# Two transformer blocks on one core: sums formed with the last products, an input split by halves, loads moved up, work taken off GpSimd

## The chip, the cores and the metric

The kernel runs on one core of a Trainium2 chip. The metric is the device time of one execution in microseconds, lower is better. TensorE (PE) multiplies matrices into PSUM; VectorE (DVE), ScalarE (ACT) and GpSimd (POOL) work element by element; SyncE (SP) issues the DMA transfers. Each engine works through its own list of instructions in order and waits for others by semaphores.

## The reference, cut to what matters

Two blocks follow each other on one sequence of 1024 positions with 1024 features, all in float32.

```python
def first_block(x, ...):                 # one layer
    z = h @ w_in[i]                      # u_pool | q | k | v
    y_pool = pool_mixer(u_pool, w_pool[i], pool_scale[i])   # per group of 128 columns: mean over
                                         # the last 2, 4, 8, 16 positions minus u, then a matmul
    y_attn = sliding_window_attention(q, k, v, attn_sinks[i])
    h = layer_norm(ALPHA * h + concat([y_pool, y_attn]) @ w_out[i])
    h = layer_norm(ALPHA * h + square(relu(h @ w_ff1[i])) @ w_ff2[i])
    return h + sigmoid(h @ w_ple_gate[i] + b) * (p[i] @ w_ple[i])

def hybrid_layer(x, ...):                # one layer, then rms_norm(x) * final_g
    h = modulate(rms_norm(x), shift_mix, scale_mix)
    qa, ka, va, qb, kb, vb = split(h @ w_in)
    oa = chunked_rel_attention(qa, ka, va, rel_bias)
    ob = stick_breaking_attention(qb, kb, vb)
    x = x + gate_mix * (concat([rms_norm(oa) * g_a, rms_norm(ob) * g_b]) @ w_out)
    gate, val = split(causal_depthwise_conv(modulate(rms_norm(x), ...) @ w_up))
    return x + gate_ffn * ((silu(gate) * val) @ w_down)
```

## The kernel before, in words

**Numbers in two parts.** Every float32 operand of a large matmul is kept as a high part (the value rounded to the format fp32r, which TensorE multiplies fast) and a low part (the value minus its high part). A product takes three matmuls: high by high, high by low, low by high. So each operand needs a split: one copy for the high part and one subtraction for the low part. For weights `prep` (line 519) loads a raw tile by SP, lets GpSimd make the high part (`split_h`, line 511) and VectorE, or the engine given as `low`, the low part. `Stream` (line 536) keeps a ring of weight slots full; its `done` frees a slot and calls for the next weight.

**Order of the work.** The kernel doesn't issue its instructions as they stand. [...] Whenever an engine is free it takes among the instructions that are ready the one that stands first in the program. The order so found is issued; waits are then set by what reads and writes what. All instructions therefore carry one line of the profile, L393, and groups are told apart by the names of their tiles. `follows` and `link` (line 250) tell the planner that a new tile lies in the memory of an old one and must come after it.

**Block 1, first part.** x comes transposed in two halves of columns. Four pooling groups follow (`pool_group`, line 748): a unit of the projection (`unit_T`), whose PSUM results ScalarE copies into `u`, then one to four sums of `u` with itself shifted by 1, 2, 4, 8 columns on VectorE, each with a short copy of the first columns (1, 2, 4, 8 of them) on GpSimd, then d = mean - u, its split (high part on GpSimd), and a small matmul (`pool_matmul`). The buffers `sc` for u, the sums and d are a ring of three. Then k, v, and four pairs of heads of attention (`attn1`, line 886), in which GpSimd normalizes the probabilities. From the third weight on all low parts of the weight stream were made by GpSimd (`ws.low = POOL`, line 724).

**v of block 2.** `wino_N` (line 1080) multiplies 1024 by 1024 matrices by Strassen's scheme in Winograd's form: seven products of half matrices. With `parts` = 1 it is used for v of both attentions. Its sequence is j = 1, 2, 5, 7, 6, 4, 3, each in two halves of the inner dimension (x = 0, 1), 14 elements in all; an element needs two operands (`prep_el`), prepared three ahead. After x = 1 four PSUM banks are copied by ScalarE to the tiles `xs(j, tp)`, tp = 0 to 3. When all are there, `gather` (line 1378) forms the results: x6 += x1, x7 += x6, x3 += x6, x3 += x5, x5 += x7, x4 += x7, x7 = x2 + x1, for each tp three sums on GpSimd and four on VectorE. Eight stores to `d_v` follow.

**q and k of block 2.** Their input h3 (eight tiles of 128 by 1024) is split tile by tile (`split_h3`, line 1465): k = 0 to 3 into the tiles `ga` from a hook that runs two elements before the end of v's products, k = 4 to 7 into slots 0 to 3 after them. `start_T` (line 971) computes the first q and k unit, first for columns 0 to 511 of both, then for 512 to 1023, calls for the next two weights, and the stage is flushed. The next stage (`p7`) loads the relative bias, evacuates these units (`q_evac`, `k_evac2`), and runs eight pairs of heads, each with its q and k unit.

**Down projection.** `wino_N` with two parts covers inner tiles 0 to 15 of 22. The last six are plain products in two sets: four tiles (`sets[0]`), then tiles 20 and 21 (`sets[1]`). In the first set, for each of eight row tiles in the order 0, 4, 1, 5, 2, 6, 3, 7, there is a product, `gather` for rows 0 to 3, a load of the residual `d_x` into a raw tile, and res = (res + product) * gate + residual. The tiles 20 and 21 are loaded by `load_k`: the activation `d_r` (split by ScalarE and VectorE) and the weight (multiplied by the gate and split by GpSimd, low part by VectorE). They were called at rows 1 and 3, that is at the third and the seventh of the eight steps, from a ring of two raw tiles which the residuals use as well.

Of the kernel before, what the change touches and what calls it, by code (L numbers as in the profile page):

```python
# [9 lines left out]
F32 = mybir.dt.float32  # L10
F32R = mybir.dt.float32r
AF = mybir.ActivationFunctionType
ALU = mybir.AluOpType
# [6 lines left out]
NT = S // P  # L20
# [14 lines left out]
def f32(ap):  # L35
    return ap.bitcast(F32)
# [51 lines left out]
class Recorder:  # L88
# [161 lines left out]
    def link(self, idx):  # L250

        op = self.ops[idx]
        if op["eng"] == "SYNC":
            op["deps"], op["cost"] = set(self.watch.get(op["watch"], ())), 0.0
            return
        eng, name, args, kw = op["eng"], op["name"], op["args"], op["kw"]
        aps = [(None, x) for x in args if isinstance(x, bass.AP)] + [(k, x) for k, x in kw.items() if isinstance(x, bass.AP)]
        outs, ins = [], []
        for i, (k, x) in enumerate(aps):
            (outs if (k in ("out", "accum_out") or (k is None and i == 0)) else ins).append(x)  # L260
        if not outs:
            raise ValueError(name)
        deps = set()
        for x in ins:
            key, cells = self.region(x)
            tab = self.cells.setdefault(key, {})
            for c in cells:
                w, r = tab.setdefault(c, [None, []])
                if w is not None:
                    deps.add(w)  # L270
                r.append(idx)
        for x in outs:
            key, cells = self.region(x)
            tab = self.cells.setdefault(key, {})
            for c in cells:
                w, r = tab.setdefault(c, [None, []])
                if w is not None:
                    deps.add(w)
                deps.update(r)
                tab[c] = [idx, []]  # L280
        for x in ins + outs:
            key = x.tensor.name
            self.watch.setdefault(key, []).append(idx)
            if key in self.alias:
                deps.add(self.alias[key])
        deps.update(op["gate"])
        deps.discard(idx)
        if eng == "SP":
            n = 4 * self.size(outs[0]) * (outs[0].ap[0][1] if "DRAM" not in str(outs[0].space).upper() else 1)
            nbytes = 4  # L290
            for _, c in list(outs[0].ap):
                nbytes *= c
            parts = max(outs[0].ap[0][1] if "DRAM" not in str(outs[0].space).upper() else 128, 1)
            cost = nbytes / 360.0 * max(1.0, 128 / parts)
        else:
            cost = self.cost(eng, name, args, kw, outs, ins)
        op["deps"], op["cost"] = deps, cost

        wide = sum("PSUM" not in str(x.space).upper() and self.size(x) > 1 for x in ins) > 1
        op["port"] = (eng == "POOL" or (eng == "DVE" and wide)) and self.size(outs[0]) > 16  # L300
        op["kind"] = None
        if eng == "PE":
            op["kind"] = "T" if name == "transpose" else "R" if ins[1].dtype == F32R else "V"
# [104 lines left out]
def two_blocks_kernel(ctx: ExitStack, tc: tile.TileContext, a, out, dbg=None):  # L408
# [34 lines left out]
    def life(pool, tag, dt, shape=(P, 2, 2, 1024)):  # L443

        t = pool.tile(list(shape), dt, tag=tag, name=uniq(tag))
        if tag in groups:
            rec.follows(t, groups[tag])
        groups[tag] = t
        return t

    def lives(tag, dt):

        return [x[:, i] for n in (0, 1) for x in [life(pers, f"{tag}{n}", dt)] for i in (0, 1)]
# [11 lines left out]
    d_v = dram.tile([NT, P, 1024], F32, name="d_v")  # L465
# [45 lines left out]
    def split_h(dst, src):  # L511
        POOL.tensor_scalar(dst, src, 1.0, 1.0, ALU.mult, ALU.mult)
# [208 lines left out]
    ws.feed(cuts=(0, 512, 1024))  # L721
    for k in range(2, KD):
        load_xT(k, 0)
    ws.low = POOL
    for k in range(KD):
        load_xT(k, 1)
    SP.dma_start(cst, a["cols"])
# [20 lines left out]
    def pool_group(g_):  # L748
        win = 2 << g_
        u = p1f()  # L750
        unit_T(g_, xT, lambda n, sl, g: ACT.copy(u[:, sl], g))
        cur, sh = u, 1
        while sh < win:
            nx = p1f()
            DVE.tensor_tensor(nx[:, sh:], cur[:, sh:], cur[:, :S - sh], ALU.add)
            POOL.tensor_copy(nx[:, :sh], cur[:, :sh])
            cur, sh = nx, sh * 2
        d = p1f()
        w1 = win - 1
        DVE.scalar_tensor_tensor(d[:, w1:], cur[:, w1:], 1.0 / win, u[:, w1:], ALU.mult, ALU.subtract)  # L760
        DVE.tensor_tensor(d[:, :w1], cur[:, :w1], cst[:, C_INV:C_INV + w1], ALU.mult)
        DVE.tensor_tensor(d[:, :w1], d[:, :w1], u[:, :w1], ALU.subtract)
        ds = Uslots[2 + g_ % 2]
        split_h(ds[:, 0, :], d)
        DVE.tensor_tensor(ds[:, 1, :], d, f32(ds[:, 0, :]), ALU.subtract)
        return ds

# [203 lines left out]
    def start_T(act, i0, units):  # L971

        gs = [ps_G() for _ in range(units)]
        for n in (0, 1):
            for j in range(units):
                gemm_T_half(gs[j][:, halves[n]], ws.slot(i0 + j), act, n)
        ws.done(units)
        return gs


# [99 lines left out]
    def wino_N(parts, a_src, b_src, R_raw, R_tmp, fx, wxf, first, els, hooks):  # L1080

        held = not hasattr(a_src, "rearrange")
        R_el = Ring([slot(i) for i in els])
        hs = lambda t: [t[:, 0:512], t[:, 512:1024]]
# [73 lines left out]
        def prep_el(i):  # L1161
            s, j, x = seq[i]
            el[i] = [element(get(s, x, n)) for n in pairs[j]]
# [3 lines left out]
        for i, (s, j, x) in enumerate(seq):  # L1167
            ea, eb = el.pop(i)
            if x == 0:
                bk = [View.of(R_8, uniq("bk")) for _ in range(4)]  # L1170
            for tp in range(4):
                for k in range(2):
                    at = slice(512 * k + tp * P, 512 * k + tp * P + P)
                    bt = slice(512 * k, 512 * k + 512)
                    PE.matmul(bk[tp], ea[:, 0, at], eb[:, 0, bt], start=(x == 0 and k == 0), stop=False)
                    PE.matmul(bk[tp], ea[:, 0, at], eb[:, 1, bt], start=False, stop=False)
                    PE.matmul(bk[tp], ea[:, 1, at], eb[:, 0, bt], start=False, stop=(x == 1 and k == 1))
                if x == 1:
                    if s == 0:
                        ACT.copy(xs(j, tp), bk[tp])  # L1180
                    else:
                        DVE.tensor_tensor(xs(j, tp), bk[tp], xs(j, tp), ALU.add)
            if i + 3 < len(seq):
                prep_el(i + 3)
            if len(seq) - 1 - i in hooks:
                hooks[len(seq) - 1 - i]()
        return xs
# [163 lines left out]
    def load_k(k, act, weight, kind="N", *more):  # L1351
        load_acts([act], [d_r[k]])
        prep(weight, (kind, pre["w"][k * P:(k + 1) * P, :]) + more)
# [108 lines left out]
    ta, tb = life(ff, "ra", F32), life(ff, "rb", F32)  # L1462
    tmps = [x[:, i // 2, i % 2] for x in (ta, tb) for i in range(4)]

    def split_h3(k):
        if k in (0, 2):
            life(pers, f"ga{k // 2}", F32R)
        dst = h3T(k)
        ACT.copy(dst[:, 0], h3r[k])
        DVE.tensor_tensor(dst[:, 1], h3r[k], f32(dst[:, 0]), ALU.subtract)  # L1470

    def early():
        for k in range(4):
            split_h3(k)

    xs = wino_N(1, h3p, a["w_v2"], [Ring(lives("ga", F32))] * 2, Ring(tmps), fx, wxf,
                {1: fxt, 2: resx[0]}, [0, 1, 2, 3, 4, 5], {2: early})
    ga = [slot(10 + k) for k in range(4)]
    for k in range(4, 8):
        split_h3(k)  # L1480
    ws = Stream([slot(4), slot(5)], [("T", w_in2[12 * br + 4 * part + i]) for br, i in order for part in range(2)])
    for tp in range(4):
        gather(tp, xs)
        for t in (tp, tp + 4):
            SP.dma_start(d_v[t], res[t])
    raws[0] = Ring(wr)
    gqkv = start_T(h3T, 0, 2)
    gu = lives("gu", F32R)
# [18 lines left out]
        return View.of(R_F, uniq("p7F"))  # L1507

    raws[0] = Ring(wr)


    rel = a["rel_bias_2"][0]
# [210 lines left out]
    gu, ga, rb = lives("gu", F32R), pre["ga"], pre["rb"]  # L1723
    rf = life(f2, "ra", F32)
    gf, fg = bc(rf[:, 0, 0], d_ada[5]), bc(rf[:, 0, 1], a["final_g_2"])
    raws[0] = Ring([rf[:, 1, 0], rf[:, 1, 1]])
    sets = [([rb[:, 0], ga[0], ga[2], slot(4)], [rb[:, 1], ga[1], ga[3], slot(5)]),
            ([gu[0], gu[2]], [gu[1], gu[3]])]
    for c in (0, 1):
# [4 lines left out]
        for t in order_t:  # L1734
            g = ps_G()
            if not last:
                gemm_N(g, acts_of(sa, t), sw)
                if t < 4:
                    gather(t, xs)
                    if t % 2:  # L1740
                        load_k(20 + t // 2, sets[1][0][t // 2], sets[1][1][t // 2], "NS", lambda: gf)
                raw = raw_tile()
                SP.dma_start(raw, d_x[t])
                DVE.tensor_tensor(res[t], res[t], g, ALU.add)
                POOL.tensor_tensor(res[t], res[t], gf, ALU.mult)
                DVE.tensor_tensor(res[t], res[t], raw, ALU.add)
                continue
# [80 lines left out]
```

## Time and profile before

| | |
|---|---|
| median of 3 runs | 2329.62 us (2328.8 to 2330.93) |
| profiled execution | 2334.03 us, span 2332.3 us |
| TensorE busy | 2233.1 us (96%) |
| VectorE busy | 1775.5 us (76%) |
| ScalarE busy | 1109.0 us (48%) |
| GpSimd busy | 663.8 us (28%) |
| mean granted TensorE clock | 0.985 |
| DMA | 304.53 MB, mean 131 GB/s |

The span runs from the first to the last instruction of the program in the profiled execution; busy time counts an engine's instructions and not its waits. PE is TensorE's matmuls; their ends are modelled. A releaser is the instruction or transfer whose end set a waiting instruction free. [...]

### The profile page before, as it was taken

What the parts mean: (1) busy time and instruction counts of PE and PEld (TensorE: products, weight loads), DVE (VectorE), ACT (ScalarE), POOL (GpSimd) and SP (SyncE); (2) the same over time, 40 slices, a digit from 0 to 9 for tenths busy, and PEclk for the clock granted to TensorE, in tenths of its full rate; (3) what the DMA queues carried; (4) which work ended last, traced back from release to release, by engine and by line L of the source; (5) the groups of instructions that cost most, each with busy time, mean ns of one, the idle gap of its engine ahead of it and who ended that gap; (6) DMA issues with size and microseconds to landing.
All of it is one profiled execution on the core that took longest, in us unless ns stands there. A gap on an engine that the chain in (4) does not pass through costs nothing.

```text
span 2332.3 us, 30737 instructions
## 1 busy us (share of the span) xinstructions
PE 2233.1 (96%) x11201; PEld 1828.5 (78%) x11201; DVE 1775.5 (76%) x2604; ACT 1109.0 (48%) x1975; POOL 663.8 (28%) x541
## 2 busy tenths in 40 slices
PE   7998999999999999999989999989899999999996
PEld 5777878777778888887877888768688888887885
DVE  6474497887677899947878887664887777779897
ACT  3264185455554340155556766431855555545412
POOL 5443200000033243624535543252000000013365
PEclk9999999999999999999999999999999999999998
DMA  6539145776542315232043333373322222244023
GB/s 199 154 96 340 60 140 208 260 251 205 197 184 89 129 59 195 73 108 82 33 144 89 89 104 89 107 241 112 109 87 85 82 82 82 82 151 165 28 99 135
DMA packets 110615, 304.53 MB, mean 131 GB/s; under 512 B 11424, under 2 KB 22912, under 8 KB 107520
## 3 DMA queue, kind: packets, MB, share of 16 engines
q1 hardware_dynamic: 110464, 302.57, 39.2%
q8 instruction: 88, 1.44, 0.2%
q14 instruction: 63, 0.52, 0.1%
HBM read 211.26 MB, written 74.49 MB: 123 GB/s over the span
## 4 chain that ended last, share of the span: by engine, by line
PE 77%; DVE 11%; DMA 5%; ACT 2%; POOL 2%; issue 2%; SPq 0%; POOLq 0%; DVEq 0%; ACTq 0%
PE PS L393 77%; DVE Q L393 4%; DVE low L393 2%; ACT Q L393 1%; POOL low L393 1%; DMA kl<-kl 1%; DVE bn L393 1%; DMA gu<-lt 1%; DMA wr<-in_w_in_dram 1%; DMA gu<-d_r 1%; POOL Q L393 1%; DMA sc<-in_xT_dram 1%; ACT gu L393 0%; DVE ga L393 0%; DVE wr L393 0%
## 5 line engine op out<-in xcount | busy, mean ns | idle before, releaser
L393 PE MATMUL PS<-low 128*128 128x512 f32 x2868 | 688.5, 393 | 7.9 <-ACT low L393 3.6
L393 PEld LDWEIGHTS PS<-low 128*128 128x128 f32 x2868 | 536.5, 189 | 123.0 <-ACT low L393 7.6
L393 PE MATMUL PS<-ga,low 128*128 128x512 f32 x1488 | 389.7, 401 | 17.8 <-ACT ga L393 7.3
L393 PEld LDWEIGHTS PS<-ga,low 128*128 128x128 f32 x1488 | 279.2, 192 | 74.9 <-issue 10.0
L393 POOL TENSOR_TENSOR ra<-ga 128x1024 f32<-128x1024 f32 x9 | 25.2, 2806 | 771.0 <-DMA ga<-in_w_down_dram 415.8
L393 ACT COPY Q<-PS 128x512 f32<-128x512 f32 (+1 forms) x312 | 174.2, 567 | 70.1 <-PE PS L393 69.5
L393 PE MATMUL PS<-gu,low 128*128 128x512 f32 x744 | 176.2, 390 | 7.4 <-POOL gu L393 7.4
L393 PEld LDWEIGHTS PS<-gu,low 128*128 128x128 f32 x744 | 139.9, 188 | 37.3 <-POOL gu L393 8.3
L393 ACT CAST low<-Q 128x512 fp32r<-128x512 f32 (+1 forms) x148 | 94.3, 639 | 138.7 <-PE PS L393 105.5
L393 PE MATMUL PS<-low,gu 128*128 128x512 f32 (+2 forms) x640 | 148.5, 384 | 2.1 <-DMA gu<-lt 1.3
L393 DVE SCALAR_TENSOR_TENSOR fy<-Q,cst,fy 128x1023 f32<-128x1023 f32 (+1 forms) x88 | 116.8, 1330 | 39.9 <-ACT fy L393 39.0
L393 DVE TENSOR_TENSOR low<-Q,low 128x512 fp32r<-128x512 f32 (+1 forms) x148 | 106.8, 723 | 39.7 <-ACT low L393 38.7
L393 PEld LDWEIGHTS PS<-low,gu 128*128 128x128 f32 x640 | 115.9, 188 | 26.2 <-issue 1.7
L393 DVE TENSOR_TENSOR low<-ra,low 128x1024 fp32r<-128x1024 f32 x76 | 107.9, 1442 | 18.7 <-ACT low L393 17.6
L393 PE MATMUL PS<-ra,low 128*128 128x512 f32 x480 | 119.6, 397 | 2.5 <-ACT ra L393 1.9
L393 DVE TENSOR_TENSOR Q<-PS,Q 128x512 f32<-128x512 f32 x162 | 108.9, 685 | 13.7 <-PE PS L393 12.6
L393 ACT CAST low<-ra 128x1024 fp32r<-128x1024 f32 x72 | 73.8, 1052 | 85.0 <-PE PS L393 66.9
L393 PE MATMUL PS<-rb,low 128*128 128x512 f32 x468 | 112.6, 389 | 0.8 <-DVE Q L393 0.8
L393 PEld LDWEIGHTS PS<-ra,low 128*128 128x128 f32 x480 | 91.5, 191 | 23.1 <-ACT ra L393 2.3
L393 DVE TENSOR_TENSOR low<-wr,low 128x512 fp32r<-128x512 f32 (+1 forms) x99 | 85.8, 869 | 30.4 <-ACT low L393 15.8
L393 POOL TENSOR_SCALAR low<-wr 128x1024 fp32r<-128x1024 f32 (+1 forms) x45 | 55.6, 1236 | 169.9 <-PE PS L393 123.0
L393 PEld LDWEIGHTS PS<-rb,low 128*128 128x128 f32 x468 | 87.8, 188 | 19.5 <-DVE Q L393 1.3
(275 smaller groups left out, 4230.8 us busy)
## 6 DMA issues: line engine op xcount, KB each, us to landing
d_r<-Q SPq DMA_DIRECT2D x32, 512.0 KB
Q<-in_w_up_dram SPq DMA_DIRECT2D x28, 512.0 KB
d_o<-oh SPq DMA_DIRECT2D x24, 512.0 KB
d_x<-Q SPq DMA_DIRECT2D x24, 512.0 KB
fxt<-in_w_ada_dram SPq DMA_DIRECT2D x48, 256.0 KB
fx<-in_w_ada_dram SPq DMA_DIRECT2D x48, 256.0 KB
wr<-in_w_in_dram SPq DMA_DIRECT2D x22, 512.0 KB
d_r<-fy SPq DMA_DIRECT2D x22, 512.0 KB
```

Of the source, the lines that this page charges most:

```text
L393: op["ins"] = op["fn"](*op["args"], **op["kw"])
```

## The change

Nine places change. The planner's `link` lets a memory handed on twice depend on the first handing on. In block 1 the weights' low parts go to VectorE, the pooling groups' short copies and the high part of d to ScalarE. `start_T` no longer calls for the next two weights; that is done after the flush. In `wino_N` with one part, the products j = 6, 4, 3 are added to a tile by VectorE as they leave PSUM, and the other sums follow on VectorE after elements 10 and 11 of 0 to 13; `gather` is not called for v. `split_h3` works on one half of the columns at a time. In the down projection the raw ring gets a third tile, and `load_k` is called at rows 0 and 1, the first and the third step.

```diff
@@ link
             op["deps"], op["cost"] = set(self.watch.get(op["watch"], ())), 0.0
+            if op["watch"] in self.alias:
+                op["deps"].add(self.alias[op["watch"]])
@@ block 1
-    ws.low = POOL
...
-            POOL.tensor_copy(nx[:, :sh], cur[:, :sh])
+            ACT.copy(nx[:, :sh], cur[:, :sh])
...
-        split_h(ds[:, 0, :], d)
+        ACT.copy(ds[:, 0, :], d)
@@ start_T
-        ws.done(units)
         return gs
@@ wino_N
                 if x == 1:
-                    if s == 0:
+                    if parts == 1 and j in (6, 4, 3):
+                        DVE.tensor_tensor(xs(j, tp), bk[tp], xs({6: 1, 4: 7, 3: 6}[j], tp), ALU.add)
+                    elif s == 0:
                         ACT.copy(xs(j, tp), bk[tp])
                     else:
                         DVE.tensor_tensor(xs(j, tp), bk[tp], xs(j, tp), ALU.add)
             if i + 3 < len(seq):
                 prep_el(i + 3)
+            if parts == 1 and i in (10, 11):
+                for tp in range(4):
+                    for u, v, w in ((7, 7, 6), (6, 6, 5), (5, 5, 7)) if i == 10 else ((7, 2, 1),):
+                        DVE.tensor_tensor(xs(u, tp), xs(v, tp), xs(w, tp), ALU.add)
@@ q and k of block 2
-    def split_h3(k):
-        if k in (0, 2):
-            life(pers, f"ga{k // 2}", F32R)
+    def split_h3(k, sl):
         dst = h3T(k)
-        ACT.copy(dst[:, 0], h3r[k])
-        DVE.tensor_tensor(dst[:, 1], h3r[k], f32(dst[:, 0]), ALU.subtract)
+        ACT.copy(dst[:, 0, sl], h3r[k][:, sl])
+        DVE.tensor_tensor(dst[:, 1, sl], h3r[k][:, sl], f32(dst[:, 0, sl]), ALU.subtract)
     def early():
+        lives("ga", F32R)
         for k in range(4):
-            split_h3(k)
+            split_h3(k, halves[0])
...
     for k in range(4, 8):
-        split_h3(k)
+        split_h3(k, halves[0])
     ws = Stream([slot(4), slot(5)], ...)
-    for tp in range(4):
-        gather(tp, xs)
-        for t in (tp, tp + 4):
-            SP.dma_start(d_v[t], res[t])
+    for k in range(8):
+        split_h3(k, halves[1])
+    for t in range(NT):
+        SP.dma_start(d_v[t], res[t])
...
     rec.flush(*gqkv)
...
     raws[0] = Ring(wr)
+    ws.done(2)
@@ down projection
-    raws[0] = Ring([rf[:, 1, 0], rf[:, 1, 1]])
+    raws[0] = Ring([rf[:, 1, 0], rf[:, 1, 1], wxf2[:, 1]])
...
-                    if t % 2:
-                        load_k(20 + t // 2, sets[1][0][t // 2], sets[1][1][t // 2], "NS", lambda: gf)
+                    if t < 2:
+                        load_k(20 + t, sets[1][0][t], sets[1][1][t], "NS", lambda: gf)
```

## Rows read from the trace of the kernel before

**Rows 1.** The page, part 4: shares of the chain that ended last.
```profile
PE 77%; DVE 11%; DMA 5%; ACT 2%; POOL 2%; issue 2%; SPq 0%; POOLq 0%; DVEq 0%; ACTq 0%
```
**Rows 2.** What TensorE waited for: us in total, times, longest us.
```profile
PE PS L393 <- POOL gu L393: 13.3, 3, 5.8
```
**Rows 3.** Stretches: length, busy us by engine (instructions), granted clock, DMA share, GB/s.
```profile
75.00:90.00 15.00, 10.46 (x39) 8.16 (x38) 7.89 (x9) 3.23 (x5) 7.78 (x6) 0.89 0.49 140
1125.00:1154.00 29.00, 29.00 (x129) 24.02 (x128) 21.68 (x13) 15.97 (x22) 24.29 (x13) 1.00 0.07 18
1182.00:1190.00 8.00, 8.00 (x32) 6.56 (x33) 5.00 (x9) 1.36 (x6) 0.62 (x3) 0.80 0.92 216
2245.00:2289.00 44.00, 44.00 (x196) 36.44 (x195) 41.46 (x32) 2.11 (x2) 25.72 (x12) 1.00 0.26 84
2289.00:2299.00 10.00, 4.28 (x19) 3.20 (x18) 6.38 (x4) 0.00 (x0) 8.45 (x4) 0.95 0.36 105
2299.00:2306.00 7.00, 6.87 (x19) 5.42 (x20) 5.00 (x7) 2.01 (x6) 1.37 (x2) 0.59 0.26 78
```
**Rows 4.** Timeline, 33 to 51: start us, us, instruction, [idle before <- releaser].
```profile
33.08 1.94 DVE L393 SCALAR_TENSOR_TENSOR sc<-sc 128x1023 f32<-128x1023 f32 x1
...
35.86 3.01 PE L393 MATMUL PS<-ga,low 128*128 128x512 f32 x12 [2.43 <-ACT sc L393]
...
40.83 2.02 POOL L393 TENSOR_SCALAR gu<-sc 128x1024 fp32r<-128x1024 f32 x1
...
42.90 0.73 PE L393 MATMUL PS<-gu,low 128*128 128x512 f32 x2 [2.90 <-POOL gu L393]
...
47.67 3.02 PE L393 MATMUL PS<-ga,low 128*128 128x512 f32 x12 [1.53 <-DVE low L393]
```
**Rows 5.** Timeline, 60 to 84.
```profile
60.41 1.22 DVE L393 SCALAR_TENSOR_TENSOR sc<-sc 128x1017 f32<-128x1017 f32 x1
...
66.31 1.32 DVE L393 TENSOR_TENSOR sc<-sc 128x1023 f32<-128x1023 f32 x1 [2.01 <-ACT sc L393]
...
77.55 2.34 POOL L393 TENSOR_TENSOR low<-wr,low 128x1024 fp32r<-128x1024 f32 x1
77.80 3.16 DVE L393 SCALAR_TENSOR_TENSOR sc<-sc 128x1009 f32<-128x1009 f32 x1
...
82.44 1.02 PE L393 MATMUL PS<-gu,low 128*128 128x512 f32 x2 [4.54 <-POOL gu L393]
```
**Rows 6.** GpSimd's groups, 18 to 235: count, busy us, mean ns, idle before.
```profile
L393 POOL TENSOR_TENSOR low<-wr,low 128x1024 fp32r<-128x1024 f32 x15 | 38.9, 2594 | 1.2
```
**Rows 7.** The page, part 5: groups of instructions, whole span.
```profile
L393 DVE TENSOR_TENSOR Q<-PS,Q 128x512 f32<-128x512 f32 x162 | 108.9, 685 | 13.7 <-PE PS L393 12.6
L393 ACT CAST low<-ra 128x1024 fp32r<-128x1024 f32 x72 | 73.8, 1052 | 85.0 <-PE PS L393 66.9
```
**Rows 8.** VectorE's groups, 1154 to 1176.
```profile
L393 DVE TENSOR_TENSOR Q<-Q,Q 128x512 f32<-128x512 f32 x8 | 5.5, 692 | 0.3
```
**Rows 9.** Timeline, 1148 to 1187.
```profile
1148.61 2.31 DVE L393 TENSOR_TENSOR low<-wxf,low 128x1024 fp32r<-128x1024 f32 x1
...
1172.48 1.17 SPq L393 DMA_DIRECT2D pT<-in_rel_bias_dram  x1
...
1178.50 0.93 DVE L393 COPY pT<-pT 8x127 f32<-8x127 f32 x1 [4.81 <-DMA pT<-in_rel_bias_dram]
...
1182.00 4.48 PE L393 MATMUL PS<-ga,low 128*128 128x512 f32 x12 [6.07 <-DVE wr L393]
```
**Rows 10.** Timeline, 2295 to 2300.
```profile
2295.61 2.34 POOL L393 TENSOR_TENSOR ra<-ra 128x1024 f32<-128x1024 f32 x1 [1.46 <-DMA ra<-in_w_down_dram]
2298.03 1.04 POOL L393 TENSOR_SCALAR gu<-ra 128x1024 fp32r<-128x1024 f32 x1
2299.13 20.63 PE L393 MATMUL PS<-gu 128*128 128x512 f32 x78 [5.85 <-POOL gu L393]
```
**Rows 11.** Waits of all engines, whole span: us in total, times, longest us.
```profile
DVE low L393 <- POOL low L393: 14.4, 7, 5.3
```

More of the change, by code (lines that the diff above doesn't have):

```diff
@@ L1463, in two_blocks_kernel @@
     tmps = [x[:, i // 2, i % 2] for x in (ta, tb) for i in range(4)]
-    def split_h3(k):
-        if k in (0, 2):
-            life(pers, f"ga{k // 2}", F32R)
+    def split_h3(k, sl):
         dst = h3T(k)
-        ACT.copy(dst[:, 0], h3r[k])
-        DVE.tensor_tensor(dst[:, 1], h3r[k], f32(dst[:, 0]), ALU.subtract)
+        ACT.copy(dst[:, 0, sl], h3r[k][:, sl])
+        DVE.tensor_tensor(dst[:, 1, sl], h3r[k][:, sl], f32(dst[:, 0, sl]), ALU.subtract)
     def early():
+        lives("ga", F32R)
         for k in range(4):
-            split_h3(k)
-    xs = wino_N(1, h3p, a["w_v2"], [Ring(lives("ga", F32))] * 2, Ring(tmps), fx, wxf,
+            split_h3(k, halves[0])
+    wino_N(1, h3p, a["w_v2"], [Ring(lives("ga", F32))] * 2, Ring(tmps), fx, wxf,
                 {1: fxt, 2: resx[0]}, [0, 1, 2, 3, 4, 5], {2: early})
```

## The prediction

> **What bounds the kernel now.** I read the chain of waits first: 77% of the chain that ended last is TensorE's own matmuls, so only time in which TensorE stands or runs slowly can be won [rows 1]. Next the list of what TensorE waits for: the dearest entry is GpSimd's output `gu`, three waits with 13.3 us in sum, two of them in block 1 and one near the end [rows 2]. [...] Last the timelines around the places that the change touches. There the reader is to see which instruction TensorE waited for, and what stood ahead of that one on its own engine.
>
> **Block 1: low parts, short copies and the split of d leave GpSimd.** TensorE waits four times in the pooling groups: 2.43 us (35.86), 2.90 (42.90), 1.53 (47.67) [rows 4] and 4.54 (82.44) [rows 5]. GpSimd is behind two of them: each weight's low part takes it 2.59 us (x15) [rows 6], and the short copies and the split of d queue behind those. VectorE suffers too: a sum over 1009 columns took 3.16 us, begun 0.25 us after a GpSimd low part, where one over 1017 columns took 1.22 [rows 5].
> - 42.90: d of group 0 was split only at 40.83. Without GpSimd beside it the sum of 33.08 takes 1.22 for 1.94, so d is there at about 34.7 (two tiny operations, some 0.4 as an estimate), and ScalarE's cast (1.05 [rows 7]) ends at 35.7. The wait goes: 2.9 (at least 2.0, if ScalarE does the two copies of the next group first).
> - 35.86: the PSUM copy in question waits for the buffer that this same sum frees: 1.94 - 1.22 = 0.7 (0 if a weight's low part is put ahead).
> - 47.67: TensorE waits for VectorE's low part of a pooled output. VectorE gets the weights' low parts on top, yet the group comes several us earlier; I take 1.0 of 1.53 (0 to 1.53).
> - 82.44: from group 3's first sum (66.31 [rows 5]) to the end of its split passed 16.1 us. Alone it is four sums and the final one at 1.22, tiny operations 0.4 and the cast 1.05: 7.6. With three weights' low parts (3.7) and four PSUM operations (2.7 [rows 7]) in VectorE's queue it is 14.0. So between 2.1 and all 4.54 goes; I take 4.0, as the matmuls ahead come sooner too. Behind this wait the stretch 75 to 90 ran at 0.89: 15 x 0.11 = 1.65 [rows 3]; I take 1.5 (0 to 1.65).
> Sum: 2.9 + 0.7 + 1.0 + 4.0 + 1.5 = 10.1, between 4.1 and 13.0.
> The rest of the 15 low parts, about eight, fall into attention. They cost VectorE 8 x 1.22 = 9.8 us and give back 8 x 2.59 = 20.7 of GpSimd, which also normalizes the probabilities. On TensorE that is between 9.8 lost, if each stood ahead of a row maximum that TensorE needs, and a few us won; I take 0, because TensorE has the next head's projection to run meanwhile.
> [...]
>
> **v's sums.** Removed: 12 evacuations by ScalarE, 12 sums by GpSimd, and the 16 sums by VectorE which ran behind the last product. Added on VectorE: 12 evacuations that add (0.685 each with a PSUM input [rows 7]) and 16 sums (0.692 [rows 8]), nearly all before the last product ends.
> [...]
> Gain: TensorE stands 6.07 us until 1182.00. VectorE had the needed PSUM reads in its queue behind a copy of `pT` that waited 4.81 us for the load of the relative bias [rows 9]. On SP that load follows the eight stores of v, which follow the sums. With the sums done some ten us sooner, stores and load move up as much, the copy runs near 1168, and the reads are done before TensorE finishes its two units (1176). Behind the wait 1182 to 1190 ran at 0.80, 1.6 us [rows 3]. Together 7.7. The two weight loads that now follow the flush are also behind the stores on SP, ahead of the bias load; slot 4 is free only near 1170, so they cost nothing. If that cover is gone, TensorE waits for one load.
> Loss: what is late next is VectorE. From 1125 to 1154 it was busy 21.7 of 29 us in 13 instructions [rows 3]; at 1.22 each, without GpSimd's sums beside them, these are 15.9. Added: 12 x 0.685 + 16 x 0.692 = 19.3, and about 0.7 because halves cost more than wholes. 35.9 us do not go into 29: an overrun of 6.9. In the program's order the first q weight's low part (1148.61 [rows 9]) comes after evacuations and sums, and TensorE wants it from its third matmul behind v. Some of the queue can be late without harm (k = 4 to 7 of the input is wanted 3 us later), so I charge 3.0, between 0 (low part put ahead, neighbouring VectorE instructions overlapping) and 9.7 (the overrun, the second weight behind the one raw buffer, a spell of low clock). The input split by halves keeps it from being more: only its first 512 columns are wanted at once. Net 7.7 - 3.0 = 4.7, between -2 and 7.7.
>
> **Down projection.** TensorE waits 5.85 us at 2299.13, because the last weight landed at 2295.6 and then needs GpSimd's product (2.34) and split (1.04) [rows 10]; the low clock behind it costs 7 x 0.41 = 2.87 [rows 3]. With three raw buffers and both loads called from the first and third step, these instructions (two loads, two GpSimd products, two splits, four casts and low parts) fall between 2245 and 2270; what is queued behind them on GpSimd, the gate products, is wanted from 2289 on. So up to 8.7 goes. What is late next is again VectorE, busy 41.5 of 44 us before 2289 [rows 3]. If it sets the end, only its own idle time goes: 10 - 6.4 in 2289 to 2299 and 7 - 5.0 after: 5.6. I take 8.0, nearer to TensorE's account, as VectorE's moved low parts also leave the tail.
>
> The edit in `link` adds no instruction; it only lets the planner see an order. The order of all engines is planned anew, which can shift any stage by some us either way.
>
> **The sum.** 10.1 + 4.7 + 8.0 = 22.8. The profiled execution took 2334.03 us (span 2332.3), 4.4 above the median of the runs; from it 2311.2, from the median of 2329.62 thus 2306.8: I say 2307.
>
> **Rivals.**
> - Everything goes, nothing new comes: 13.0 + 7.7 + 8.7 = 29.4, 2300. For it: TensorE's low clock only follows waits. Against it: the VectorE count.
> - VectorE sets v's seam and the end: 10.1 - 2 + 5.6 = 13.7, 2316. For it: both stretches fill VectorE. Against it: 13 rows there were drawn out by GpSimd, which stops.
> - The early gains are given back in the attentions, which have VectorE chains of their own, and only the down projection's 8.0 stays: 2322. Against it: no wait of TensorE in attention is among the dear ones.
> - Slower: the weights' low parts now wait on VectorE. Each needs GpSimd's high part, and this waits for TensorE to free a slot. On GpSimd nothing stood behind such a wait; on VectorE the softmax does. Seven such waits of VectorE are in the trace, 14.4 us, 2.06 each [rows 11]. At that price the 15 low parts cost 30.9, and the time is 2329.6 - 22.8 + 30.9 = 2338. It decides from 22.8 / 15 = 1.5 us each on TensorE's path. Against it: TensorE has other work beside most of them.
>
> **Chances.** Forecast 0.48, all goes 0.18, VectorE sets both 0.18, given back 0.07, slower 0.05, near no change 0.04. Below 0.2% (4.7 us) a measurement of this kernel can't tell from none. So faster 0.91, same 0.04, slower 0.05. The range, 2296 to 2320, takes in the first three.
>
> **What would show it.** Right: no wait above 1 us for GpSimd's `gu` up to 90 us; the wait before the second q unit gone; no stand of TensorE between the two sets of the down projection, and 1.00 clock there. Wrong: a new wait for VectorE's low part where the first q unit begins, longer than 5 us; more idle TensorE in either attention; an end that VectorE sets. If VectorE's waits for GpSimd's `low` grow by over 20 us in block 1, the slower rival is right.

## The result, and the profile after

The changed kernel takes 2307.46 us (median of 4 runs, 2304.0 to 2309.92); the kernel before, on the same chip, 2330.27 (4 runs). The medians differ by 22.8 us; the ratio is 0.9897 [0.9882, 0.9911], by which it is 24.0 us [20.7, 27.5]. Forecast were 2307 and 22.8. The profiled execution took 2306.23 us, its span is 2304.4, and TensorE's mean granted clock, the share of full speed that it was given, 0.987 (before 0.985).

The chain of waits, shares of the span (answers to [rows 1]):
```profile
PE 80%; DVE 11%; issue 3%; ACT 3%; DMA 2%; POOL 1%; SPq 0%; DVEq 0%; POOLq 0%; ACTq 0%
```
The dearest of what TensorE waits for, whole span (us in total, times, longest us):
```profile
PE PS L395 <- DVE low L395: 8.4, 5, 3.2
PE PS L395 <- DVE m L395: 7.7, 11, 1.9
PE PS L395 <- ACT Q L395: 7.1, 5, 3.6
```
GpSimd's `gu`, the dearest entry before [rows 2], is gone from this list, and so is the 6.07 us wait for `wr` [rows 9]. Nothing above 8.4 took its place.

The stretches that answer to [rows 3] (behind the length the busy us of TensorE, its weight loads, VectorE, ScalarE and GpSimd; then granted clock, DMA share, GB/s): block 1, v's last products, the start of q, the second q unit, and the end:
```profile
75.00:90.00 15.00, 15.00 (x71) 12.42 (x70) 2.75 (x3) 2.35 (x4) 1.05 (x1) 1.00 1.03 292
1110.00:1139.00 29.00, 28.42 (x126) 23.21 (x124) 27.14 (x39) 12.06 (x18) 1.36 (x1) 1.00 0.24 97
1139.00:1145.00 6.00, 3.94 (x10) 2.86 (x11) 6.00 (x10) 0.50 (x1) 0.00 (x0) 0.73 0.96 340
1161.00:1169.00 8.00, 7.82 (x38) 6.29 (x37) 6.17 (x9) 2.27 (x6) 2.43 (x3) 1.00 0.58 129
2266.00:2290.00 24.00, 22.48 (x98) 17.86 (x96) 23.66 (x32) 8.46 (x23) 15.67 (x12) 1.00 0.22 78
```
75 to 90 is without a gap and at a granted clock of 1.00. VectorE is full before v's end (27.14 of 29, 39 instructions for 13), and TensorE has a new loss at 1139, with the low clock behind it. At the end VectorE is full (23.66 of 24).

One pair of executions must not be read too closely. The two profiled ones differ by 27.9 us in span, the medians by 22.8. Comparing the time of one and the same TensorE instruction, an execution with block 1 unedited (the down edit alone, below) was already 2.3 us ahead of the profiled one of before at 60 us, all of it by 20 us, where no edit shows yet, and 5.6 at 224; and between two executions of the changed kernel itself, the stretch 1480 to 1520 differed by 4.0.

### The profile page after: what moved, and what is told of

Read it like the earlier page. It is cut to its first block, busy times and chain, and to the rows that moved or that the text cites. A ratio compares the mean times of both kernels' runs of the same rounds, so it can differ in the third digit from the quotient of the medians.

```text
span 2304.4 us, 30724 instructions
## 1 busy us (share of the span) xinstructions
PE 2231.7 (97%) x11201; PEld 1826.1 (79%) x11201; DVE 1789.2 (78%) x2643; ACT 1107.0 (48%) x1985; POOL 588.7 (26%) x496
## 4 chain that ended last, share of the span: by engine, by line
PE 80%; DVE 11%; issue 3%; ACT 3%; DMA 2%; POOL 1%; SPq 0%; DVEq 0%; POOLq 0%; ACTq 0%
PE PS L395 80%; DVE Q L395 4%; DVE low L395 2%; ACT Q L395 1%; DMA gu<-d_r 1%; ACT gu L395 1%; DVE e L395 1%; DVE gu L395 0%; DVE fxt L395 0%; ACT low L395 0%; DVE wr L395 0%; DVE m L395 0%; DMA v<-d_ada 0%; DVE fs L395 0%; DVE fy L395 0%
## 5 line engine op out<-in xcount | busy, mean ns | idle before, releaser
L395 ACT COPY Q<-PS 128x512 f32<-128x512 f32 (+1 forms) x304 | 169.5, 567 | 60.8 <-PE PS L395 60.3
L395 DVE TENSOR_TENSOR low<-wr,low 128x512 fp32r<-128x512 f32 (+1 forms) x118 | 109.8, 934 | 52.1 <-POOL low L395 37.4
L395 DVE TENSOR_TENSOR low<-ra,low 128x1024 fp32r<-128x1024 f32 x76 | 104.6, 1399 | 14.6 <-ACT low L395 14.5
```

What stands on the lines that cost most here:

```text
L395: op["ins"] = op["fn"](*op["args"], **op["kw"])
```

## The experiments

**Each part alone** (e1_block1, e1_v, e1_down), and the whole beside them (e1_all). Each kernel is the one before with one group of edits of the change above: block 1's three lines; v's sums, the input by halves, the edit in `link` and the moved `ws.done`; or the down projection's third raw buffer and earlier loads:
```diff
-    ws.low = POOL                                          # e1_block1
-            POOL.tensor_copy(nx[:, :sh], cur[:, :sh])
+            ACT.copy(nx[:, :sh], cur[:, :sh])
-        split_h(ds[:, 0, :], d)
+        ACT.copy(ds[:, 0, :], d)
...
+                    if parts == 1 and j in (6, 4, 3):       # e1_v
...
-                    if t % 2:                               # e1_down
+                    if t < 2:
...
```


> Block 1's three edits alone (low parts to VectorE, short copies and the split of d to ScalarE), all else as before. [...] Rival (low parts on VectorE hold up the softmax): 5 us or less, with TensorE later again by 224 us. The changed kernel also came 3.3 us earlier between 289 and 445 us, where nothing was edited; if that belongs to block 1's edits, it is here as well, 13 to 16 us in all.

> The edits around v alone (sums formed with the last products, input split by halves, next weights called after the flush, the planner's link). My theory: 4 to 6 us below before; the 6.07 us wait before the second q unit goes, about 3 us of new waits stand where the first q unit begins. Rival: the gain in the changed kernel was only the new order of the attention behind it, then the sign can be either and the time is within 2 us of before.

> The earlier loads and the third raw buffer in the down projection alone. My theory after the result: TensorE ends 6.8 us earlier, yet VectorE sets the end, so the time falls by 5 us. Rival (the term of my sum as it stood): 8 us.

> The changed kernel again, beside its parts. If the three parts act in places that don't touch each other, its gain is the sum of the three within 3 us, about 23. If a new order of the attentions makes up much of it, the sum misses by more than 5.

Measured on one chip (before 2331.53, 22 runs):

| kernel | median, runs | ratio | us less |
|---|---|---|---|
| e1_block1 | 2320.03, 6 | 0.9954 [0.9940, 0.9968] | 10.7 [7.5, 14.0] |
| e1_v | 2324.36, 11 | 0.9974 [0.9965, 0.9984] | 6.1 [3.7, 8.2] |
| e1_down | 2325.67, 12 | 0.9973 [0.9963, 0.9983] | 6.3 [4.0, 8.6] |
| e1_all | 2306.86, 5 | 0.9901 [0.9885, 0.9917] | 23.1 [19.3, 26.8] |

The parts add up: 10.7 + 6.1 + 6.3 = 23.1. Forecast were 10.1, 4.7 and 8.0. Each interval takes in its forecast, so the times alone correct none of the three terms; the traces do, below. The gain between 289 and 445 us that I had asked after is in e1_block1's trace (3.7 us from 300 to 450), but 3.0 of it are given back by 700.

**Which edit of block 1 it was** (e2_low_pool, e2_short_pool): the changed kernel with one edit undone each.
```diff
+    ws.low = POOL                                           # e2_low_pool
...
-            ACT.copy(nx[:, :sh], cur[:, :sh])               # e2_short_pool
+            POOL.tensor_copy(nx[:, :sh], cur[:, :sh])
-        ACT.copy(ds[:, 0, :], d)
+        split_h(ds[:, 0, :], d)
```


> The changed kernel with one thing of block 1 undone: the low parts of its stage go back to GpSimd, while the short copies and the split of d stay on ScalarE. Block 1's edits alone gave 10.7 us (7.5 to 14.0). Theory: the low parts are the load, because they stood ahead of what TensorE waits for on GpSimd (a low part 2.39 to 2.59 us there, and VectorE's own operations drawn out beside it), so at least 5 us come back: 2312 to 2316 us, a ratio to the kernel before of 0.992 to 0.9935, and waits of TensorE for GpSimd's gu are seen again between 33 and 84 us. Rival: the short copies on GpSimd were the load, and GpSimd with the low parts alone is early enough: at most 2 us come back, 2307 to 2309 us, and no wait of TensorE for GpSimd over 0.5 us.

> The changed kernel with the other thing of block 1 undone: the short copies and the split of d go back to GpSimd, the low parts stay on VectorE. Theory (the low parts were the load): GpSimd has room for the short copies, at most 2 us come back: 2307 to 2309 us, a ratio of 0.990 to 0.991. Rival (the short copies were the load): at least 5 us come back, 2312 us or more, with TensorE's waits for GpSimd's gu seen again between 33 and 84 us.

Measured (before 2332.96): e2_low_pool 2317.23, ratio 0.9936 [0.9921, 0.9952], 14.9 us less than before, so 8 to 9 of the 23 to 24 us came back. e2_short_pool 2308.9, 0.9893 [0.9880, 0.9906]: nothing came back. The low parts are the load; that the short copies left GpSimd is worth nothing measurable once the low parts have gone.

With the low parts alone back on GpSimd TensorE has no wait for GpSimd's `gu`, against what I had expected: ScalarE writes `gu` there. TensorE waits for ScalarE, which waits for VectorE. Timeline of e2_low_pool, 30 to 37:
```profile
30.85 3.19 POOL L395 TENSOR_TENSOR low<-wr,low 128x1024 fp32r<-128x1024 f32 x1
31.87 3.24 DVE L395 SCALAR_TENSOR_TENSOR sc<-sc 128x1023 f32<-128x1023 f32 x1
...
35.03 0.98 DVE L395 TENSOR_TENSOR sc<-sc,cst 128x1 f32<-128x1 f32 x1
35.22 0.58 ACT L395 COPY sc<-PS 128x512 f32<-128x512 f32 x1 [5.03 <-DVE sc L395]
35.95 1.66 PE L395 MATMUL PS<-ga,low 128*128 128x512 f32 x4 [4.20 <-ACT sc L395]
```
The changed kernel at the same work, 31 to 35:
```profile
31.38 1.21 DVE L395 SCALAR_TENSOR_TENSOR sc<-sc 128x1023 f32<-128x1023 f32 x1
32.52 0.15 DVE L395 TENSOR_TENSOR sc<-sc,cst 128x1 f32<-128x1 f32 x1
...
32.75 0.59 ACT L395 COPY sc<-PS 128x512 f32<-128x512 f32 x1 [3.64 <-DVE sc L395]
33.11 1.22 DVE L395 TENSOR_TENSOR low<-wr,low 128x1024 fp32r<-128x1024 f32 x1
33.23 1.04 ACT L395 CAST gu<-sc 128x1024 fp32r<-128x1024 f32 x1
...
34.42 0.71 PE L395 MATMUL PS<-gu,low 128*128 128x512 f32 x2 [0.97 <-ACT gu L395]
```
The same sum takes 3.24 us beside a GpSimd low part and 1.21 alone, and ScalarE's copy, which needs its buffer, comes late (e2_low_pool 35.22, the changed kernel 32.75). The same low part took 3.19 us on GpSimd and takes 1.22 on VectorE.

So there are two costs, and both need the low parts on GpSimd: VectorE's operations are drawn out (left alone in e2_low_pool), and the short copies and d's split queue behind the low parts (the waits for `gu` of [rows 4, 5], which need both edits undone). The traces say what each is worth, if the same TensorE instruction is compared from 20 us, where no edit shows yet, to 113 us. Ten executions with the low parts on VectorE agree there within 0.1 us, e2_short_pool among them. Against the changed kernel e2_low_pool loses 6.4, and the three with block 1 unedited lose 11.5 to 12.1 (the kernel before 11.9). So the first cost is some 6.4 us, low clock behind its waits included, and the second 5.1 to 5.7. By the medians the second is 14.9 - 6.1 - 6.3 = 2.5, with intervals of 3 us at each term. From 120 to 2245 us e2_low_pool lost 5.2 more, but e3_raw_pool (below), which has the low parts on VectorE, lost 5.4 there as well, so nothing is read from that.

**What q's start waits for** (e2_late7, e3_pool7, e3_after7). In the changed kernel, timeline 1136 to 1151:
```profile
1137.53 0.68 DVE L395 TENSOR_TENSOR Q<-PS,fxt 128x512 f32<-128x512 f32 x1
...
1138.73 0.68 DVE L395 TENSOR_TENSOR Q<-PS,fxt 128x512 f32<-128x512 f32 x1
1139.33 1.28 DVE L395 TENSOR_TENSOR low<-gu,low 128x512 fp32r<-128x512 f32 x2
1139.46 0.73 PE L395 MATMUL PS<-ga,low 128*128 128x512 f32 x2 [1.04 <-DVE Q L395]
1140.53 1.21 DVE L395 TENSOR_TENSOR low<-wxf,low 128x1024 fp32r<-128x1024 f32 x1
1141.66 1.28 DVE L395 TENSOR_TENSOR ga<-gu,ga 128x512 fp32r<-128x512 f32 x2
...
1141.79 4.13 PE L395 MATMUL PS<-ga,low 128*128 128x512 f32 x10 [1.60 <-DVE low L395]
```
TensorE waits for the last eviction of v, which frees the PSUM bank that it needs, and for the first q weight's low part; both stand in VectorE's queue. The sum x7 = x2 + x1 (four operations) was moved back: behind the first-half splits, then onto GpSimd, then behind the opening of q, with v's stores.
```diff
-                    for u, v, w in ((7, 7, 6), (6, 6, 5), (5, 5, 7)) if i == 10 else ((7, 2, 1),):
+                    for u, v, w in ((7, 7, 6), (6, 6, 5), (5, 5, 7)):
...
+    for tp in range(4):                 # e2_late7: here; e3_pool7: here, POOL; e3_after7: behind start_T
+        DVE.tensor_tensor(xs(7, tp), xs(2, tp), xs(1, tp), ALU.add)
     for k in range(8):
         split_h3(k, halves[1])
...
```


> The changed kernel with v's sum x7 formed behind the splits of the first q half, not in the step of v's last product but one, so that VectorE has four operations of 0.69 us (2.8 us) less ahead of the first q weights' low part and of the bank that TensorE waits for. Theory: the 1.2 and 1.8 us that TensorE loses where q starts are VectorE's queue, not a transfer: both fall, together by 2 to 3 us, and the stretch at the low clock behind them (1.7 us lost) shortens: 2 to 4 us under the changed kernel, 2303 to 2305 us. Rival: the queue is only shifted, and the sums moved hold TensorE later, at the second q half: no difference, 2306 to 2308 us, with a new wait of TensorE for VectorE at that place.

> v's sum x7 is formed on GpSimd (four operations of about 1.3 us), behind the splits of the first q half, where the kernel with x7 only shifted back (on VectorE) still loses 1.0 us to a bank, because two of its four sums stand between VectorE's evictions of v's last product. Theory: the bank is late by those two sums alone (2 x 0.69 us), so the 1.0 us wait goes too: about 1 us under the kernel with x7 shifted, 2303 to 2305 us on a chip where the kernel before takes 2330. Rival: VectorE and GpSimd draw each other's operations out (a sum on VectorE of 2.3 to 3.4 us beside GpSimd instead of 1.2 was seen in the down projection), the evictions come later and the wait grows: 1 to 3 us more, 2306 to 2309 us.

> v's sum x7, and v's stores with it, stand behind the opening of the q stream, so that no sum lies between the evictions of v's last product. Theory: TensorE's wait of 1.0 us for the bank goes, as with x7 on GpSimd, and nothing is drawn out: 2303 to 2305 us. Rival: the sums are put between the evictions all the same, since they are ready, or the stores of v come so late that the first attention waits for v: no gain, 2305 to 2308 us, with that wait shown.

Measured: e2_late7 2305.2, 0.9880 [0.9867, 0.9893]; e3_pool7 2307.21, 0.9896 [0.9878, 0.9913]; e3_after7 2308.89, 0.9901 [0.9888, 0.9915]. Against the changed kernel's 0.9897 and 0.9901 e2_late7 has the lowest ratio, but the intervals overlap: the times show no gain. Its trace gained 3.5 us on the profiled execution of the changed kernel between 1087 and 1176, and so did that of e3_raw_pool (below), which has the same edit: the 1.60 wait is gone, the clock stays at 1.00, the 1.0 for the bank stays, since two of the four sums, and now the low part too, stand between the evictions. Of the two waits that I had expected to fall, one did. It came from VectorE's queue, and from no transfer.

Not all of the 3.5 belongs to the edit. e1_all, the changed kernel once more, has the same two waits and no low clock behind them. Its timeline, 1137 to 1150:
```profile
1141.54 0.73 PE L395 MATMUL PS<-ga,low 128*128 128x512 f32 x2 [1.04 <-DVE Q L395]
1143.88 2.56 PE L395 MATMUL PS<-ga,low 128*128 128x512 f32 x10 [1.60 <-DVE low L395]
```
The ten matmuls take 2.56 us where they took 4.13, and e1_all gains 1.6 us over the same stretch without any edit. Against it e2_late7 gains 1.9, which is the wait alone.

e3_pool7 missed: the bank's wait fell to 0.6, but the wait for the low part came back (1.6). Its timeline, 1132 to 1146:
```profile
1135.32 3.17 DVE L395 TENSOR_TENSOR ga<-gu,ga 128x512 fp32r<-128x512 f32 x2
...
1136.20 3.45 POOL L395 TENSOR_TENSOR Q<-wxf,wr 128x512 f32<-128x512 f32 x2
...
1143.24 1.22 DVE L395 TENSOR_TENSOR low<-wxf,low 128x1024 fp32r<-128x1024 f32 x1
```
Two splits of the input take VectorE 3.17 us beside GpSimd's sums and 1.28 in e2_late7, and the low part stands behind the evictions again, where e2_late7 has it between them. VectorE's work is drawn out, as the rival said.

e3_after7 has no wait at q's start and gains 4.8 us on the changed kernel between 1087 and 1154 (1.6 of them by the low clock that it lacks), yet only 1.2 of that is left at 1240. Its timeline, 1146 to 1161, with v's last four stores and the loads behind them:
```profile
1148.53 2.86 SPq L395 DMA_DIRECT2D d_v<-Q  x4
...
1151.48 2.42 SPq L395 DMA_DIRECT2D wr<-in_w_in_dram  x2
...
1154.06 0.30 SPq L395 DMA_DIRECT2D pT<-in_rel_bias_dram  x1
...
1157.59 1.05 POOL L395 TENSOR_SCALAR low<-wr 128x1024 fp32r<-128x1024 f32 x1 [12.75 <-DMA wr<-in_w_in_dram]
...
1158.67 1.23 DVE L395 TENSOR_TENSOR low<-wr,low 128x1024 fp32r<-128x1024 f32 x1 [2.54 <-POOL low L395]
1159.81 0.21 DVE L395 COPY pT<-pT 8x127 f32<-8x127 f32 x1
```
and what its TensorE waited for, 1120 to 1260:
```profile
PE PS L395 <- DVE Q L395: 2.5, 1, 2.5
PE PS L395 <- DMA gu<-wr: 0.5, 1, 0.5
```
The bias is loaded at 1154 where the changed kernel loads it at 1148, and the 2.5 us wait stands in the first attention, at 1209, as the kernel before had one of 2.92. Timeline of the kernel before, 1220 to 1235:
```profile
1229.84 3.34 PE L393 MATMUL PS<-cst,Q 128*128 128x128 f32 x13 [2.92 <-DVE Q L393]
```
Its rival, late stores, was right that the gain is lost, though the wait shown is not for v. Which of the loads behind the stores does it is not shown: the copy of the bias (1159.81) starts without a wait for its load, right behind a low part that waited for a weight from the same queue.

**What sets the end** (e2_tail, e3_tail_out, e3_raw_pool). e2_tail gives the second half of each final tile to ScalarE alone and leaves out final_g there; e3_tail_out stores that half unscaled, leaving out scale and final_g; e3_raw_pool has x7 as e2_late7 and gives four of the eight sums with the stored tile to GpSimd.
```diff
-                    DVE.scalar_tensor_tensor(z[:, sl], res[t][:, sl], r, fg[:, sl], ALU.mult, ALU.mult)
+                    ACT.activation(z[:, sl], res[t][:, sl], AF.Copy, scale=r)               # e2_tail
...
+                SP.dma_start(out[0, t * P:t * P + P, sl], (z, res[t])[n][:, sl])              # e3_tail_out
...
+                (DVE if t < 4 else POOL).tensor_tensor(res[t], res[t], raw, ALU.add)          # e3_raw_pool
```


> The changed kernel with the second half of each final tile scaled on ScalarE by its own reciprocal alone, so that VectorE has one operation of each tile less in the last 60 us; it leaves out the multiplication of that half by final_g. Theory: VectorE sets the end of the changed kernel (the down projection gave back 5 of the 6.8 us that TensorE gained there): the end comes 3 to 6 us earlier, 2301 to 2304 us, and the waits of TensorE for VectorE's Q behind 2270 us are gone. Rival: TensorE's last products or the stores of the output set it: at most 1 us, 2306 to 2308 us.

> The changed kernel with the second half of each final tile stored without its scaling and without final_g (both left out), so that VectorE has eight operations of 0.70 to 1.5 us less in the last 40 us and no other engine has more. Theory: VectorE sets the end, and the trial that gave these operations to ScalarE only moved the limit there: the end comes 2 to 4 us earlier, 2302 to 2305 us, and the stretch behind TensorE's last product falls from 14.5 us to 11 or 12. Rival: the chain of one tile behind the last product (eviction, squares, mean, scaling, store) sets it: at most 1 us, 2306 to 2308 us, with the stretch still over 13.5 us.

> The kernel with x7 shifted back, and in the down projection's first set of products the last sum of four of the eight tiles (the tile stored earlier is added to it) on GpSimd instead of VectorE. Theory: VectorE sets the end of the down projection, full from 2222 to 2298 us with 94 of 102 us less the stores; four sums of 1.2 to 3.1 us less bring its end forward by 3 to 6 us, of which the waits of TensorE for VectorE's Q (1.5 us) and the sums left behind TensorE's last product are what can be had: 2 to 5 us under the kernel with x7 shifted, 2300 to 2303 us. Rival: GpSimd's added sums draw VectorE's out, or come too late for the second set: no difference or slower, 2304 to 2309 us.

Measured: e2_tail 2306.74, 0.9887 [0.9872, 0.9902]; e3_tail_out 2304.72, 0.9884 [0.9870, 0.9897]; e3_raw_pool 2307.78, 0.9896 [0.9881, 0.9911]. The times don't separate them; the last stretch does. 2290 to 2310 of the changed kernel, of e2_tail and of e3_tail_out, columns as in the table of stretches above:
```profile
2290.00:2310.00 20.00, 0.28 (x2) 0.00 (x0) 8.27 (x17) 7.10 (x17) 6.17 (x8) 0.72 0.38 144
```
```profile
2290.00:2310.00 20.00, 0.98 (x5) 0.48 (x3) 4.89 (x10) 10.14 (x24) 7.23 (x9) 0.66 0.38 143
```
```profile
2290.00:2310.00 20.00, 2.02 (x9) 1.33 (x8) 4.51 (x12) 6.81 (x17) 6.70 (x8) 0.75 0.42 160
```
From the start of TensorE's last matmul to the end of the span pass 14.6, 14.4 and 10.9 us. e2_tail took work from VectorE (8.27 to 4.89) and loaded ScalarE as much (7.10 to 10.14): nothing won of the 3 to 6 us expected, and the trial told little. With the work on neither engine 3.7 us go. The last evictions say where. The changed kernel, timeline 2291 to 2299:
```profile
2291.30 2.20 DVE L395 SCALAR_TENSOR_TENSOR wr<-Q,rmr,ra 128x512 f32<-128x512 f32 x2
...
2293.68 1.87 DVE L395 TENSOR_TENSOR Q<-Q,PS 128x512 f32<-128x512 f32 x3
```
and e3_tail_out, 2291 to 2296:
```profile
2291.98 1.28 DVE L395 TENSOR_TENSOR Q<-Q,PS 128x512 f32<-128x512 f32 x2
```
From the start of TensorE's last matmul to the end of VectorE's last eviction pass 5.7 us in the changed kernel and 1.6 in e3_tail_out; from there to the end of the span 8.9 and 9.3. So VectorE's queue ahead of the last evictions sets 4 us of the end. What follows them, the chain that the rival named with its stores, takes the other 9, and no trial shortened it. In e2_tail the two parts are 2.2 and 12.2: ScalarE took what VectorE gave up.

e3_raw_pool lost 4.0 us between 2245 and its last products, in an execution of 2316.05 us, the slowest of its five; its timeline, 2262 to 2292:
```profile
2268.64 8.54 POOL L395 TENSOR_TENSOR Q<-Q,ra 128x1024 f32<-128x1024 f32 x3 [4.14 <-DVE Q L395]
...
2271.52 3.41 DVE L395 TENSOR_TENSOR Q<-Q,wxf 128x1024 f32<-128x1024 f32 x1
...
2274.85 3.60 DVE L395 TENSOR_TENSOR Q<-Q,Q 128x512 f32<-128x512 f32 x2
...
2280.56 11.65 PE L395 MATMUL PS<-gu 128*128 128x512 f32 x50 [3.45 <-DVE Q L395]
```
Its four sums less on VectorE are paid for by what is left there: one sum of 3.41 us beside GpSimd, two of 0.7 in 3.60. The rival was right.

## Why the prediction was right, and where it was not

- **Block 1**, forecast 10.1, measured 10.7 [7.5, 14.0] by the medians and 11.5 to 12.1 by the traces up to 113 us. The waits of 2.90, 1.53 and 4.54 are gone, that at 35.86 too; one of 0.97 is left at 34.42, and 75 to 90 ran at 1.00. The sum that I put at 1.22 without GpSimd beside it takes 1.21. What I had underrated are the drawn-out VectorE operations: I charged them 0.7 of the sum at 35.86, where the whole wait of 2.43 went, and they alone cost 6.4 us in e2_low_pool. My upper bound of 13.0 was not the sum of my terms either: as I had bounded them they add up to 11.3, and 13.0 has the whole 2.43 in it. The low parts in attention, which I put at 0, show nothing clear: from 113 to 224 us the three executions without these edits gained 1.6 and 1.0 and lost 0.9 against the changed kernel.
- **v's seam**, net 4.7 forecast, 6.1 [3.7, 8.2] measured, with terms that fell apart differently. The wait of 6.07 and its low clock went. The loss by waits was 2.97 (at 1139.46 and 1141.79, from the start of one matmul to the start of the next, less the 0.23 that a matmul takes), forecast 3.0. The low clock behind it, 6 x 0.27 = 1.6 at 1139 to 1145, I had only in the upper bound, and it does not come each time: behind the same waits e1_all, e1_v and e2_low_pool ran on at 1.00. Other waits had none behind them either: in the kernel before, 30 to 45, with the waits of 2.43 and 2.90, ran at 1.00, though all 19 of its 155 stretches of 15 us that ran below 1.00 hold a stand of TensorE or follow one that does. Against the loss stands what I hadn't seen: a wait of 2.92 us in the first attention, at 1229.84, is gone as well, which is worth 2.9 us between 1190 and 1240 in four executions with v's edits and nothing in e3_after7. The bias load came 24.5 us earlier (1172.48 to 1147.98) where TensorE had come 16 earlier, and v's stores and the weight loads moved up with it; which of them frees that wait is not shown. Some 2 us were given back by 1400, of which executions without the edits of v show 1.0 and 1.3 too.
- **Down projection**, 8.0 forecast, 6.3 [4.0, 8.6] measured: this is the mis-sized term. The interval of the times still holds 8.0; the traces do not. TensorE gained 6.7 us there (6.5 in e1_down; no stand between the two sets, but 1.5 of new waits for VectorE), but the end came only 4.9 earlier in e1_down and 5.1 in the two executions of the changed kernel, because the stretch from TensorE's last matmul to the end grew from 13.0 to 14.6 us: VectorE's last eviction trails by 5.7 us where it trailed by 3.6. VectorE's account, 5.6, was the nearer one, and I had taken TensorE's. That VectorE's moved low parts would leave the tail was no ground: GpSimd's products there still draw its operations out (two half tiles in 3.10 us at 2285.98 beside GpSimd, in 1.41 at 2297.94 without its products).
- **The sum** came out since the errors are of both signs: by the medians 0.6 and 1.4 too little and 1.7 too much, all inside the intervals; by the traces block 1 was some 2 too little and the down projection 3 too much. That they cancel to within 1 us is luck.
- **Slower rival.** Its test was badly chosen. VectorE's waits for GpSimd's `low` up to 240 us grew to
```profile
DVE low L395 <- POOL low L395: 23.6, 6, 9.2
```
from 5.3, by 18.3, near the 20 that I had set, and cost TensorE nothing that the trace shows: VectorE had spare time there (2.75 of 15 us busy in 75 to 90). A wait on an engine says something only with what is queued behind it. With the low parts on GpSimd it is 5.1, and the kernel is slower.

## What to carry to other kernels

When work leaves GpSimd, count first what its neighbour VectorE gets back: a sum took 3.24 us beside it and 1.21 alone, and that held the chain even where no one waited for GpSimd. Where a wait of the bottleneck is removed at the end of a kernel, take the account of the next engine, not the wait's length. And where a queue issues stores and loads in order, look also at what depends on them much later: in e3_after7 a wait came back some 60 us behind the stores that were moved.

Of the versions that compute the whole result, e2_late7 is the best by its median, though its interval overlaps the others'. x7 between the second-half splits, behind all evictions and ahead of q's opening, might take away the bank's wait as well without making v's stores late; that wasn't tried.

## What was not expected of the hardware

Between executions of one and the same program, stretches with the same instructions moved by up to 4 us (1480 to 1520, where two of the changed kernel differ by 4.0), while others agree closely (1240 to 1300, within 0.2 over all kernels). The granted clock makes much of it: 1500 to 1520 ran at 0.83 in the one execution and at 0.68 in the other, which is 3.0 of the 4.0 us, and behind the same two waits at q's start the matmuls ran at a granted clock of 0.73 in the one and of 1.00 in the other. The spread of the runs, 2304 to 2312 for one kernel, is of that size. What an edit of 2 or 3 us is worth can be read at its place, but not from one pair of spans.
